# Two 512-wide tiles for the prompt, and a token-major product for the samples, in a decoder's input projection

## The chip, the core and the metric

The kernel runs on one core of one Trainium2 chip. The core has five engines that run side by side, each through its own queue in order: TensorE (PE, matrix products into PSUM, with its weight loads as PEld), VectorE (DVE), ScalarE (ACT, activations and casts), GpSimd (POOL) and SyncE (SP), which here issues the DMAs. The metric is the time of one execution in microseconds (us).

## The reference

One layer of a decoder in fp32 with 1024 prompt tokens and 32 sample tokens (8 sequences of 4), width 1024. One input projection feeds two groups of 512 channels: an HGRN2 recurrence with four heads, and a gated depthwise convolution of width 31 with a layer norm. An output projection merges them; then come the residual and a final RMSNorm.

```python
h = rmsnorm(x, norm_g)
proj = h @ w_in                                   # 1024 -> 3584
q, fp, i, za, glu, zb = jnp.split(proj, [s1, s2, s3, s4, s5], axis=-1)
q = silu(q); f = lb + (1 - lb) * sigmoid(fp); k = 1 - f; logf = log(f)
o_a, s_new = hgrn2_chunked(heads(q), heads(k), heads(i), heads(logf), s0)
o_a = rmsnorm(o_a, a_norm_g) * silu(za)
u = (glu + b_glu)[..., :512] * sigmoid((glu + b_glu)[..., 512:])
cv, buf_new = causal_dwconv(u, conv_buf, conv_w, conv_b)
o_b = silu(layernorm(cv, ln_g, ln_b)) * silu(zb)
out = x + concatenate([o_a, o_b], -1) @ w_out     # then the final rmsnorm
```

The same layer runs over the prompt (from a zero state) and over the samples (from given states).

## The kernel before

**Input.** `prep_x` normalizes 128 tokens at a time, turns them on PE and splits them into a high and a low part (type float32r), so that three fast products, high x high, high x low and low x high, stand in for one of fp32. The result is `xT`: channels in partitions, 1056 tokens (1024 of the prompt, then the 32 samples) in columns. `xsT` keeps the 32 sample tokens unsplit. `v_block` makes the values `i` token-major; `col_tiles` makes those of the samples by plain fp32 products that place the 32 tokens in one of four groups of 32 output partitions.

**Projections.** The other 24 blocks of 128 output channels are made feature-major, in the order of `ORD` (gb, ga: the two halves of the GLU; f, q; then za, zb). `load_w` fetches a block's weights into `wraw` (two buffers), and ScalarE and VectorE split them into `wh` and `wl`. `project` runs over three tiles of MB = 352 columns (3 x 352 = 1056), 24 matmuls each (8 slices of the contraction, three products), each tile in a PSUM bank of the tag `mm` (4 banks). Then it evacuates the banks, the third first (`nbs=(2, 0, 1)`), with an activation or a VectorE operation that `evac` makes; `after` chains them, and `lnexp_after` asks for the table set of logarithm and exponential behind the last.

**What sets the order.** `pump`, called behind the first and the second tile and at the end, emits pieces of the recurrence (`hgrn`, up to HU = 3 a call) and of background work (convolution `conv`, layer norm `ln_main`), as long as VectorE's sum of estimated costs lags PE's by less than LEAD. A scheduler then orders the instructions of each engine by its own estimate of the time; the pieces marked `high_priority` come first among those that can start. Each engine's queue runs strictly in the order that results.

**Memory.** `big` tiles (4 x 1056 columns) share six buffers: four of `xT`, the split weights of `i` (later `mixa`) and `cv`; later the output weights and the residual reuse them. PSUM: `mm` 4 banks, `aux` 2, `ops` 1, `ptps` 1.

Nearly every VectorE and PE instruction goes through the helper `Clock`, so in the profile its line is L72 (L73 after the change), and tiles tell instructions apart. The recurrence of the sample tokens has a group that the prediction uses: eight plain fp32 products of `qz` (32 columns of weights) with `s0` (tag `raw`, 128 moving columns), in the four column groups, into an `aux` bank (L645 to L654); a plain fp32 product `ops<-pt,vt` (L558) is another.

Of the kernel before, what the change touches and what calls it, by code (L numbers as in the profile page):

```python
# [18 lines left out]
P = 128  # L19
# [6 lines left out]
MB = 352  # L26
KO = 8
# [17 lines left out]
# columns of the packed per-partition vectors  # L45
# [9 lines left out]
# masks: causal, then s/t pairs of each level 64..1, then the diagonal  # L55
# [33 lines left out]
def _pe_ns(name, a, k):  # L89
    rhs = k.get("rhs")  # L90
    n = _free(a[0])
    if rhs is None:
        return 109
    return max(107, n / 2.4) if rhs.dtype == F32R else max(60, 4 * n / 2.4)


def emit(nc, tc, h, fast, flag_out=None):
    HW = 6 if fast else 5
    with ExitStack() as ctx:
# [8 lines left out]
        def big(dt=F32, w=TOK):  # L108
            return pool.tile([P, 4, w], dt, tag="big", name="big", bufs=6)
# [4 lines left out]
        def mmbank():  # L114
            return bank("mm", 4)
# [19 lines left out]
        xT = [[big(F32R) for _ in range(2)] for _ in range(2)]  # [hi/lo][ko half]  # L135
# [5 lines left out]
        xsT = sb([P, KO, ST], "ho", 2)  # L141
# [11 lines left out]
        def prep_x(tb, xr, n):  # L153
            sq = sb([P, 1], "ss", 4)
            junk = sb([P, D], "hw", HW, BF16)
            S.activation(junk[0:n, :], xr[0:n, :], AF.Square, accum_out=sq[0:n, :])  # L156
            S.activation(sq[0:n, :], sq[0:n, :], AF.Ln, bias=eps[0:n, :], scale=1.0 / D)  # L157
            S.activation(sq[0:n, :], sq[0:n, :], AF.Exp, scale=-0.5)
            V.scalar_tensor_tensor(
                xr[0:n, :], xr[0:n, :], sq[0:n, :], gin[0:n, :], ALU.mult, ALU.mult  # L160
            )
            for hf in range(2):
                tp = aux() if hf else mmbank()
                for k in range(4):
                    ko = hf * 4 + k
                    T.transpose(
                        tp[:, k * n : (k + 1) * n],
                        xr[0:n, ko * P : (ko + 1) * P],
                        ident[0:n, 0:n],
                    )  # L170
                src = tp[:, 0 : 4 * n].rearrange("p (k t) -> p k t", t=n)
                hi = xT[0][hf][:, :, tb * P : tb * P + n]
                S.copy(hi, src)  # L173
                if tb == 8:
                    S.copy(xsT[:, 4 * hf : 4 * hf + 4, :], src)
# [95 lines left out]
        # queries of the sample tokens, one zero-padded group of columns for each sequence  # L271
# [8 lines left out]
        # lower bound of the forget gate: first row of the softmax over the logits  # L280
# [25 lines left out]
        def load_w(blk):  # L306
            with tc.high_priority(HP):
                wr = sb([P, KO, P], "wraw", 2)
                nc.sync.dma_start(wr, h["win"][blk])
                hi = sb([P, KO, P], "wh", 2, F32R)  # L310
                lo = sb([P, KO, P], "wl", 2, F32R)
                S.copy(hi, wr)  # L312
                V.tensor_tensor(lo, wr, hi.bitcast(F32), ALU.subtract)
            return hi, lo
# [28 lines left out]
        def pump():  # L343
            for _ in range(HU):
                step(hq)
            while bg and V.ns < T.ns + LEAD * 1000:
                step(bg)
# [35 lines left out]
        def act_into(dst, func, bias=0.0):  # L383
            def f(nb, ps):
                return [S.activation(dst[:, nb * MB : (nb + 1) * MB], ps, func, bias=bias)]  # L385
# [7 lines left out]
        def hgrn(hd, q, k, g):  # L393
# [4 lines left out]
            for hf in range(2):  # L398
# [44 lines left out]
                # decayed keys towards the chunk's end, token-major  # L443
# [155 lines left out]
            # the four groups of partitions hold the parts (hi, hi, lo, lo) of the keys and  # L599
            # (hi, lo, hi, lo) of the values, so one product carries all four pairs  # L600
# [101 lines left out]
        def conv(c, u):  # L702
# [61 lines left out]
        def glu_evac(u, func, bias):  # L764
            us = u[:, UW:UEND].rearrange("p (b t) -> p b t", t=PAD + NS)

            def f(nb, ps):
                n = min(MB, SEQ - nb * MB)
                parts = [(u[:, PAD + nb * MB : PAD + nb * MB + n], ps[:, 0:n])]
                if n < MB:  # L770
                    parts.append((us[:, :, PAD:], ps[:, n:MB].rearrange("p (b t) -> p b t", t=NS)))
# [90 lines left out]
        for i, (kind, c) in enumerate(order):  # L862
# [23 lines left out]
            elif kind == "ga":  # L886
# [8 lines left out]
                if c == 3:  # L895
# [5 lines left out]
                    bg.append(ln_main())  # L901
# [24 lines left out]
            else:  # L926
# [14 lines left out]
                elif c == 3:  # L941
# [5 lines left out]
                        (0, 1, 2),  # L947
# [22 lines left out]
        for ko in range(KO):  # L970
# [11 lines left out]
            else:  # L982
                if ko == 4:
                    hi1 = big(F32R, D)
                    lo1 = big(F32R, D)
# [13 lines left out]
        def newton(y, v):  # L999
            # one step for y = v ** -0.5; v is used up  # L1000
# [63 lines left out]
        def finish(tb, pss):  # L1064
            if tb % 4 == 0:
                xres["t"] = big(w=D)
# [28 lines left out]
        pss = [[mmbank(), mmbank()] for _ in range(2)]  # L1095
# [123 lines left out]
```

## Time and profile before

| what | value |
|---|---|
| median of 3 runs | 519.52 us (519.48 to 519.6) |
| span of the profiled execution | 517.7 us |
| median less that span | 1.8 us |
| mean granted TensorE clock | 0.990 |
| matmuls 352 wide into `mm` | 1728 |
| projections | 24 |

The page gives the span from the first to the last instruction; it has no time of its own for what lies around the span, so the runs' median stands for it. The trace tells of each instruction when it started, how long it was at work, and what ended the engine's idle time before it. Matmuls are pipelined: their durations overlap, and the distance from one start to the next is what a matmul costs the engine. A plain fp32 product is recorded as two matmuls. The chain of work is followed back from the last instruction to what released it, or to the one before it on its engine; its pieces are runs of one engine and tile. In a table of stages each row has, for PE, PEld, DVE, ACT and POOL, the busy time and the count of instructions, then the granted clock, the share of the DMA engines and GB/s.

### The profile page before, as it was taken

Reading aid. Unit: us, or ns where it says so; the run is one execution under the profiler, and the core shown is the slowest. Engines: PE = TensorE matmul, PEld = TensorE weight load, DVE = VectorE, ACT = ScalarE, POOL = GpSimd, SP = SyncE. Lnnn points to the kernel's source line nnn. Section 1 sums busy time; section 2 is a strip of 40 time slices with the busy share of each in tenths; the row PEclk is TensorE's granted clock in tenths of the full one; section 3 lists DMA queues with packets and bytes.
Section 4 is the critical chain, followed back from the end, with each engine's and each line's share of the span. In section 5 each row is a group of like instructions: output and inputs, shape, how many; then the busy total and the mean of one; then the engine's idle time right before and its main releaser. Section 6 shows DMA issues by size and latency. Waiting matters only on the chain.

```text
span 517.7 us, 8480 instructions
## 1 busy us (share of the span) xinstructions
PE 502.1 (97%) x3404; PEld 453.2 (88%) x3404; DVE 384.0 (74%) x721; ACT 275.6 (53%) x517; POOL 2.9 (1%) x20
## 2 busy tenths in 40 slices
PE   5999999999999999999999999999999999999992
PEld 5789999889999999989999999999999967788881
DVE  4872299998988369998999989979566767545432
ACT  5873343213866475654737644754757868343321
POOL 1000000000000000000000000000000000000000
PEclk9899999999999999999999999999999999999997
DMA  8734122200211204111151001221125370211111
GB/s 303 241 136 100 42 52 50 43 0 1 51 42 43 55 22 114 41 42 47 42 122 47 22 37 47 88 76 42 47 56 185 128 304 33 87 46 42 63 58 47
DMA packets 21854, 39.37 MB, mean 76 GB/s; under 512 B 10512, under 2 KB 11792, under 8 KB 21808
## 3 DMA queue, kind: packets, MB, share of 16 engines
q1 hardware_dynamic: 21808, 38.77, 24.2%
q8 instruction: 28, 0.46, 0.4%
q14 instruction: 18, 0.15, 0.1%
HBM read 31.52 MB, written 7.24 MB: 75 GB/s over the span
## 4 chain that ended last, share of the span: by engine, by line
PE 94%; DMA 2%; ACT 2%; DVE 1%; SPq 1%; issue 0%; DVEq 0%
PE mm L72 73%; PE ops L72 8%; PE ptps L72 8%; PE aux L72 5%; DMA wl<-wi 2%; ACT hw L156 1%; DVE qkg L72 0%; SPq L216 0%; ACT big L173 0%; ACT big L224 0%; SPq L150 0%; ACT ss L157 0%; ACT big L1078 0%; ACT qkg L1089 0%; DVE cq L72 0%
## 5 line engine op out<-in xcount | busy, mean ns | idle before, releaser
L72 PE MATMUL mm<-big,wh 128*128 128x352 f32 (+1 forms) x1280 | 325.0, 332 | 0.0
L72 PEld LDWEIGHTS mm<-big,wh 128*128 128x128 f32 x1280 | 224.2, 188 | 7.1 <-issue 0.4
L72 PE MATMUL mm<-big,wl 128*128 128x352 f32 (+1 forms) x640 | 212.4, 332 | 0.0
L72 PEld LDWEIGHTS mm<-big,wl 128*128 128x128 f32 x640 | 120.5, 188 | 3.8 <-issue 0.4
L72 DVE SCALAR_TENSOR_TENSOR big<-u,wsum,big 128x511 f32<-128x511 f32 (+14 forms) x60 | 44.3, 739 | 0.3
L72 DVE TENSOR_TENSOR wl<-wraw,wh 128x1024 fp32r<-128x1024 f32 x24 | 29.3, 1222 | 20.6 <-ACT wh L312 20.5
L72 DVE SCALAR_TENSOR_TENSOR big<-u,cols,big 128x511 f32<-128x511 f32 (+14 forms) x60 | 44.1, 737 | 0.0
L72 DVE SCALAR_TENSOR_TENSOR cq<-u,cols,cq 128x511 f32<-128x511 f32 (+13 forms) x56 | 41.1, 734 | 0.0
L385 ACT ACTIVATE qkg<-mm 128x352 f32<-128x352 f32 x48 | 19.2, 465 | 31.7 <-PE mm L72 31.6
L312 ACT CAST wh<-wraw 128x1024 fp32r<-128x1024 f32 x24 | 25.2, 1050 | 19.0 <-PE mm L72 10.3
L72 DVE TENSOR_TENSOR qkg<-mm,big 128x512 f32<-128x512 f32 x16 | 10.9, 689 | 30.9 <-PE mm L72 30.9
L72 DVE TENSOR_TENSOR hw<-hw,qkg 128x512 f32<-128x512 f32 (+1 forms) x64 | 32.7, 550 | 0.0
L72 PE MATMUL ops<-big 128*128 128x512 f32 (+1 forms) x128 | 26.4, 399 | 1.7 <-ACT big L224 1.7
L325 ACT ACT_TABLE_LOAD x20 | 25.7, 1283 | 0.3
L72 PE MATMUL mm<-vt,wl 128*128 128x512 f32 x64 | 25.0, 391 | 0.0
L72 PE MATMUL mm<-vt,wh 128*128 128x512 f32 x64 | 25.0, 393 | 0.0
L1078 ACT ACTIVATE big<-qkg 128x512 f32<-128x512 f32 x16 | 10.0, 628 | 23.7 <-DVE qkg L72 23.7
L72 PEld LDWEIGHTS ptps<-hw 128*32 128x32 f32 (+1 forms) x448 | 13.7, 113 | 8.6 <-issue 3.4
L72 PE MATMUL ptps<-big 128*128 128x512 f32 x64 | 20.9, 395 | 0.4 <-ACT big L173 0.4
L72 PEld LDWEIGHTS ops<-big 128*128 128x128 f32 (+1 forms) x128 | 14.8, 155 | 5.9 <-ACT big L224 1.9
L72 PE MATMUL ptps<-hw 128*32 128x32 f32 (+1 forms) x448 | 19.7, 210 | 0.0
L385 ACT ACT_TABLE_LOAD x15 | 19.2, 1283 | 0.7 <-DVE hw L72 0.4
(226 smaller groups left out, 682.0 us busy)
## 6 DMA issues: line engine op xcount, KB each, us to landing
wraw<-win SPq DMA_DIRECT2D x24, 512.0 KB, 3.7
big<-xp SPq DMA_DIRECT2D x2, 2048.0 KB, 10.0
o_yp<-qkg SPq DMA_DIRECT2D x16, 256.0 KB, 2.3
wraw<-wo SPq DMA_DIRECT2D x6, 512.0 KB, 3.8
raw<-sh SPq DMA_DIRECT2D x4, 512.0 KB, 5.5
o_hs<-raw SPq DMA_DIRECT2D x4, 512.0 KB, 2.7
wh<-xp SPq DMA_DIRECT2D x3, 512.0 KB, 10.1
raw<-xp SPq DMA_DIRECT2D x2, 512.0 KB, 5.1
```

Source lines behind the costliest of these rows:

```text
L72: return f(*a, **k)
L156: S.activation(junk[0:n, :], xr[0:n, :], AF.Square, accum_out=sq[0:n, :])
L312: S.copy(hi, wr)
L325: after(S.preload_act_table_set("natural_log_exp_and_others"), prev)
L385: return [S.activation(dst[:, nb * MB : (nb + 1) * MB], ps, func, bias=bias)]
L1078: S.activation(xr[:, hs], y[:, hs], AF.Square, accum_out=sqs[:, half : half + 1])
```

## The change

`project` now makes the prompt's 1024 columns in two tiles of TB = 512, and the 32 sample columns apart:

- Eight plain fp32 products into a bank of its own (`smp`, one buffer; `mm` has three) take the unsplit weights `w[2]` (`wraw`) as the moving operand and `xsT` as the weights, 32 tokens in each of four groups of partitions, two slices of the contraction summed in each group. The result is token-major: four partial sums of 32 tokens x 128 channels.
- ScalarE copies that to `sps`, and one fp32 product with `bones` (ones where two partitions mean the same token) sums the four parts and turns them to 128 channels x 32 tokens, in other columns of the `smp` bank.
- The third "tile" that `evac` sees is that 32-column piece. The order of evacuation is 0, 1, 2 everywhere.
- `pump` is called behind the sample group, in the second tile behind its fourth slice (after the turning product), and at the end.

`load_w` returns the unsplit weights too, so `wraw` stays in use until PE has read it. `xT` has 1024 columns and a tag of its own (`xt`, four buffers; `big` has two); the output weights and the residual that reused `big` now reuse `xt`. The sample tokens aren't split any more in `prep_x`, and `xsT` has its own tag. `step` and `pump` hold the layer norm's generator until all four heads are done. The cost estimate of a matmul gains 13 (or 10) ns. The first two output tiles of the output product use three `mm` banks and `smp`. Comments are gone, so line numbers differ.

```diff
-            return bank("mm", 4)
+            return bank("mm", 3)
+
+        def smpbank():
+            return bank("smp", 1)
...
+                if tb == 8:
+                    S.copy(xsT[:, 4 * hf : 4 * hf + 4, :], src)
+                    continue
                 hi = xT[0][hf][:, :, tb * P : tb * P + n]
                 S.copy(hi, src)
-                if tb == 8:
-                    S.copy(xsT[:, 4 * hf : 4 * hf + 4, :], src)
...
         def step(q):
-            while q:
+            while q and not (q[0] is late.get("ln") and len(hdone) < H):
...
-        def project(w, evac, ndrain, nbs=(2, 0, 1), more=()):
+        def project(w, evac, ndrain, more=()):
             pss = []
-            for nb in range(3):
+            smp = smpbank()
+            for nb in range(2):
                 ps = mmbank()
                 i = 0
                 for ko in range(KO):
                     for a, b in ((0, 0), (0, 1), (1, 0)):
                         T.matmul(
-                            ps[:, 0:MB],
+                            ps,
                             lhsT=w[b][:, ko, :],
-                            rhs=xT[a][ko // 4][:, ko % 4, nb * MB : (nb + 1) * MB],
+                            rhs=xT[a][ko // 4][:, ko % 4, nb * TB : (nb + 1) * TB],
                             start=(i == 0),
                             stop=(i == 23),
                         )
                         i += 1
+                    if nb == 1 and ko == 3:
+                        T.matmul(
+                            smp[:, P : P + ST], lhsT=sps, rhs=bones[:, 0:ST], start=True, stop=True
+                        )
+                        if ndrain:
+                            pump()
                 pss.append(ps)
-                if nb < 2 and ndrain:
-                    pump()
+                if nb == 0:
+                    for ko in range(KO):
+                        j = ko % 4
+                        T.matmul(
+                            smp[j * ST : (j + 1) * ST, 0:P],
+                            lhsT=xsT[:, ko, :],
+                            rhs=w[2][:, ko, :],
+                            start=(ko < 4),
+                            stop=(ko >= 4),
+                            tile_position=(0, j * ST),
+                        )
+                    sps = sb([P, P], "sps", 2)
+                    S.copy(sps, smp[:, 0:P])
+                    if ndrain:
+                        pump()
+            pss.append(smp[:, P : P + ST])
             with tc.high_priority(HP):
                 last = None
-                for nb in nbs:
-                    for ins in evac(nb, pss[nb][:, 0:MB]):
+                for nb in range(3):
+                    for ins in evac(nb, pss[nb]):
```

How the order of PE's queue changes, at the projection ga0 (the second one). Before, at the end of a tile (a row is a line, an operation, output<-inputs by the program's names with their numbers, and the output's shape; `mm_501` is the bank of the tile, `big` is `xT`, `wh` and `wl` the split weights, `ops` and `ptps` the banks of `v_block`):

```order
L72 MATMUL mm_501<-big_77,wh_408 128x352
L72 MATMUL mm_501<-big_77,wl_409 128x352
L72 MATMUL mm_501<-big_79,wh_408 128x352
L72 MATMUL ops_865<-qkg_164,big_77 128x512
L72 MATMUL ops_865<-big_80,big_79 128x512
L72 MATMUL ptps_891<-big_80,big_76 128x512
```

The tile ends, and other products of the same fast type follow at once. After, ga0's second tile goes into `mm_519` (`xt` is `xT`, `smp_483` the sample bank, `wraw` the unsplit weights, `xsT` the sample tokens):

```order
L73 MATMUL mm_519<-xt_76,wh_404 128x512
L73 MATMUL mm_519<-xt_76,wl_405 128x512
L73 MATMUL mm_519<-xt_78,wh_404 128x512
L73 MATMUL smp_483<-wraw_402,xsT_84 32x128 x8
L73 MATMUL mm_519<-xt_76,wh_404 128x512
L73 MATMUL mm_519<-xt_76,wl_405 128x512
L73 MATMUL mm_519<-xt_78,wh_404 128x512
```

The eight sample products stand behind the first three matmuls of the second tile. 21 matmuls of 512 columns further on, already in the first tile (`mm_560`) of the next projection, follows the product that turns them:

```order
L73 MATMUL mm_560<-xt_76,wh_479 128x512
L73 MATMUL mm_560<-xt_76,wl_480 128x512
L73 MATMUL smp_483<-bones_374,sps_517 128x32
L73 MATMUL mm_560<-xt_78,wh_479 128x512
L73 MATMUL mm_560<-xt_76,wh_479 128x512
```

So the copy to `sps` has that stretch of PE's queue to be done in. Most of the 24 projections read alike; in seven the group of eight is cut in two by other matmuls.

The other place is ScalarE's queue around the third q block (c = 2). Before (`qkg<-mm` is the evacuation of a projection, ACT_TABLE_LOAD the load of a table set):

```order
L694 ACTIVATE big<-aux,eps 128x512
L695 ACTIVATE big<-big 128x512
L385 ACT_TABLE_LOAD
L385 ACTIVATE qkg<-mm 128x352 x3
L325 ACT_TABLE_LOAD
L312 CAST wh<-wraw 128x1024
```

The three tiles are evacuated in one batch between two table loads. After, at the same projection:

```order
L727 ACTIVATE big<-ops 128x512
L421 ACT_TABLE_LOAD
L421 ACTIVATE qkg<-mm 128x512
L482 ACT_TABLE_LOAD
L482 ACTIVATE eg<-qkg 128x4
L398 COPY sps<-smp 128x128
```

The first tile is evacuated by itself, and the set of the exponential (`eg`) is loaded again before the copy and before the second tile. In the whole fast path ScalarE's queue has 44 table loads before and 79 after.

More of the change, by code (lines that the diff above doesn't have):

```diff
@@ L106, in sb, with big @@
             return pool.tile(shape, dt, tag=tag, name=tag, bufs=bufs)
-        def big(dt=F32, w=TOK):
-            return pool.tile([P, 4, w], dt, tag="big", name="big", bufs=6)
+        def big(dt=F32, w=TOK, tag="big"):
+            return pool.tile([P, 4, w], dt, tag=tag, name=tag, bufs={"big": 2, "xt": 4}[tag])
         def bank(tag, bufs):
@@ L132, in emit @@
         nc.vector.tensor_copy(avgr, av)
-        xT = [[big(F32R) for _ in range(2)] for _ in range(2)]
+        xT = [
+            [big(F32R, SEQ, "xt") for _ in range(2)]
+            for _ in range(2)
+        ]
         wih = big(F32R, D).rearrange("p a (b n) -> p (a b) n", n=512)
@@ L346, in pump @@
             while bg and V.ns < T.ns + LEAD * 1000:
+                if bg[0] is late.get("ln") and len(hdone) < H:
+                    break
                 step(bg)
-        def project(w, evac, ndrain, nbs=(2, 0, 1), more=()):
+        def project(w, evac, ndrain, more=()):
             pss = []
-            for nb in range(3):
+            smp = smpbank()
+            for nb in range(2):
                 ps = mmbank()
@@ L384, in f @@
             def f(nb, ps):
[L385 removed]
+                return [
+                    S.activation(dst[:, nb * TB : min(TOK, (nb + 1) * TB)], ps, func, bias=bias)
+                ]
             return f
@@ L900, in emit @@
                     bg.insert(len(bg) - 1, lnp())
-                    bg.append(ln_main())
+                    late["ln"] = ln_main()
+                    bg.append(late["ln"])
             elif kind == "f":
@@ L1065, in finish @@
             if tb % 4 == 0:
-                xres["t"] = big(w=D)
+                xres["t"] = big(w=D, tag="xt")
                 nc.sync.dma_start(
@@ L1094, in emit @@
         mixes = [split_mix(0), split_mix(1)]
-        pss = [[mmbank(), mmbank()] for _ in range(2)]
+        pss = [[mmbank(), mmbank()], [mmbank(), smpbank()]]
         for kos in (range(4), range(4, KO)):
```

20 lines of the change are left out of this document (10 added, 10 removed).

## The prediction

> **What bounds the kernel now.** I read the share of each engine first, then the chain of work that ended last, then what TensorE waited for.
>
> ```profile
> span 517.7 us, 8480 instructions
> PE 502.1 (97%) x3404; PEld 453.2 (88%) x3404; DVE 384.0 (74%) x721; ACT 275.6 (53%) x517; POOL 2.9 (1%) x20
> ...
> PE 94%; DMA 2%; ACT 2%; DVE 1%; SPq 1%; issue 0%; DVEq 0%
> PE mm L72 73%; PE ops L72 8%; PE ptps L72 8%; PE aux L72 5%; DMA wl<-wi 2%; ACT hw L156 1%; DVE qkg L72 0%; SPq L216 0%; ACT big L173 0%; ACT big L224 0%; SPq L150 0%; ACT ss L157 0%; ACT big L1078 0%; ACT qkg L1089 0%; DVE cq L72 0%
> ```
>
> TensorE is 94% of the chain, and matmuls into the `mm` banks are 73%: the 24 projections and the output product. A busy PE could still hide waits, so the list of PE's waits comes next.
>
> ```profile
> PE ops L72 <- ACT big L224: 1.7, 1, 1.7
> PE mm L72 <- DVE avg L132: 1.6, 1, 1.6
> PE mm L72 <- DVE raw L72: 1.2, 1, 1.2
> PE ops L72 <- DVE qkg L72: 0.8, 1, 0.8
> PE ptps L72 <- ACT big L173: 0.4, 1, 0.4
> PE mm L72 <- ACT ho L175: 0.2, 1, 0.2
> ```
>
> These six waits sum to 5.9 us and are of the input stage (L132, L173, L224 build the transposed input). The table of stages says the same of the 296 us in which most projections and all recurrences run:
>
> ```profile
> 114.00:410.00 296.00, 296.00 (x2248) 279.93 (x2248) 247.58 (x470) 179.47 (x329) 0.25 (x2) 1.00 0.20 56
> 180.00:340.00 160.00, 160.00 (x1230) 150.07 (x1229) 143.60 (x281) 96.66 (x186) 0.00 (x0) 1.00 0.21 57
> ```
>
> PE is busy for every microsecond, at the full granted clock; VectorE for 248 and ScalarE for 179. So what the change is worth is, first, what it does to the sum of PE's own spacings. Durations of single matmuls (some 330 ns) overlap and are no price; the price is the time from start to start.
>
> **The tiles.** A projection had 3 x 24 matmuls 352 wide and gets 2 x 24, 512 wide. The chain has an unbroken run of each shape:
>
> ```profile
> 56.66 22.97 PE mm L72 x144
> ...
> 449.91 58.25 PE mm L72 x256
> ```
>
> 22.97 / 144 = 159.5 ns for 352 columns, 58.25 / 256 = 227.5 ns for 512 (the output product). Before: 72 x 159.5 = 11.48 us. After: 48 x 227.5 = 10.92. That saves 0.56 us; with the starts below (160 ns between neighbours) it is 72 x 160 - 48 x 227 = 0.62. I take 0.60, or **-14.4 us** for 24 projections (13.5 to 15.0). Most comes from the 24 matmuls fewer (their fixed part: 227 - 160 = 67 ns buys 160 columns, 0.42 ns each, so 12 to 13 ns of the 160 are fixed), the rest from 32 of 1056 columns.
>
> **The sample group.** Eight plain fp32 products, weights 128x32, 128 moving columns, into four column groups. The old kernel has exactly this form in the recurrence of the sample tokens (`aux<-raw,qz`, recorded as 16, two records each), and once it stands alone among 352-wide matmuls:
>
> ```profile
> 254.88 0.32 PE L72 MATMUL mm<-big,wl 128*128 128x352 f32 x1
> 255.13 0.64 PE L72 MATMUL aux<-raw,qz 128*32 128x128 f32 x16
> 255.70 0.59 PE L72 MATMUL mm<-big,wh 128*128 128x352 f32 x2
> 256.13 0.32 PE L72 MATMUL mm<-big,wl 128*128 128x352 f32 x1
> ```
>
> From 254.88 to 256.13 are 1.25 us, in which three plain 352-wide matmuls (0.48) start too: the group costs **0.77 us**; I use 0.78. Only some 0.48 of it is the group's own records; the rest is the switch of form, paid going in (0.25 to the first record where 0.16 is usual) and coming out. The way in is no wait for data, since it is the same before other column-tiled groups:
>
> ```profile
> 153.04 0.32 PE L72 MATMUL mm<-big,wh 128*128 128x352 f32 x1
> 153.29 0.33 PE L72 MATMUL ptps<-hw 128*64 128x64 f32 x2
> ```
>
> Again 0.25. The other instance took a little more:
>
> ```profile
> 188.41 0.42 PE L72 MATMUL mm<-big,wh 128*128 128x352 f32 x1
> 188.77 0.64 PE L72 MATMUL aux<-raw,qz 128*32 128x128 f32 x16
> 189.34 0.43 PE L72 MATMUL mm<-big,wl 128*128 128x352 f32 x1
> ```
>
> 0.93 from matmul to matmul against 0.82 above: 0.88 for the upper end. 24 x 0.78 = **+18.7 us** (11.5, without any switch, to 21.1).
>
> **The turning product.** One plain fp32 product, 128x128 weights and 32 moving columns. Its nearest row alone among 352s is the fp32 product of 128 moving columns, two records:
>
> ```profile
> 277.78 0.32 PE L72 MATMUL mm<-big,wh 128*128 128x352 f32 x1
> 277.94 0.38 PE L72 MATMUL ops<-pt,vt 128*128 128x128 f32 x2
> 278.08 0.41 PE L72 MATMUL mm<-big,wh 128*128 128x352 f32 x1
> 278.33 0.32 PE L72 MATMUL mm<-big,wl 128*128 128x352 f32 x1
> ```
>
> 277.78 to 278.33 is 0.55 us; without it 0.32; so 0.23, and fewer columns need not help, since the two records start 0.11 apart. 24 x 0.225 = **+5.4 us** (0.14 to 0.30 each). The new order also cuts seven of the 24 groups in two; two pieces stand far apart and pay the switch again: 2 x 0.3 = **+0.6** (0 to 2.1).
>
> PE's sum: -14.4 + 18.7 + 5.4 + 0.6 = **+10.3 us**. The saving is smaller than the work that replaces it: 0.60 against 1.00 us a projection.
>
> A rule of the Trainium skill speaks about the fixed part: the page TensorEngine Tiling (Array Packing), section Performance Considerations, Instruction Overhead, gives every matmul about 60 cycles of overhead, 25 ns at the 2.4 GHz that it assumes. By it the tiles would save more and the sum would be some 7 us smaller; the rows of 159.5 and 227.5 ns put the fixed part at half of that, and they decide.
>
> **What lies beside PE.** ScalarE gains 24 copies of `smp`, and the evacuation changes from three of 352 to two of 512 and one of 32.
>
> ```profile
> L656 ACT COPY kts<-aux 128x128 f32<-128x128 f32 x4 | 1.0, 255 | 3.3 <-PE aux L72 3.3
> L385 ACT ACTIVATE qkg<-mm 128x352 f32<-128x352 f32 x48 | 19.2, 465 | 31.7 <-PE mm L72 31.6
> L1078 ACT ACTIVATE big<-qkg 128x512 f32<-128x512 f32 x16 | 10.0, 628 | 23.7 <-DVE qkg L72 23.7
> L325 ACT ACT_TABLE_LOAD x20 | 25.7, 1283 | 0.3
> ```
>
> A projection: 3 x 0.465 = 1.40 before; 2 x 0.628 + 0.28 + 0.26 = 1.79 after; 9 us more in all. Larger is what the order does: the first tile no longer waits for the last, so its activation is issued mid-projection, and other tables come between. ACT_TABLE_LOADs go from 44 to 79: 35 x 1.283 = 45 us. In 114 to 410 us ScalarE would go from 179 to about 230 of 303 us. It has the room: 116 us idle there, and the evacuations alone waited 31.6 us for PE. What matters is whether a late copy holds `smp<-bones,sps`, since PE's queue goes no further. The order puts that product 21 matmuls behind the group: 21 x 0.227 = 4.8 us. Before it ScalarE has, at the third q block, an activation (0.63), a table (1.28), a small exponential (0.2) and the copy (0.26): 2.4 us from the end of the first tile. Covered by 2 us; with a second table or a late VectorE operand it would not be. I price that at **+1.7 us**, about one table load and a bit exposed in all 24, with 0 and 22 us (half of the 45) as ends.
>
> The weights' raw tile is now read by PE, so the load two blocks on (SP's queue, 3.7 us) waits for the group. It was free after VectorE's split; now it is free mid-projection, with 5.4 us of that projection and the whole next one still to run before its first use. Behind it on SP stand state loads and outputs, needed later still. Three banks and a fourth suffice, since two are held and the third takes the next tile. Sample columns leave the hi/lo split of the input: four short operations fewer on ScalarE and VectorE, none of them on PE. I cost all this at nothing; if the cover went, one late weight load would cost up to its 3.7 us.
>
> The sum: 10.3 + 1.7 = **+12.0**. The profiled execution's span is 517.7; the runs' median 519.52 has 1.8 around it, which I carry unchanged: **531.5 us**.
>
> **Rivals.**
> - *ScalarE's tables surface.* Place: the recurrence stage, where VectorE too is at 143.6 of 160 us and each late exponential idles it. A third to a half of the 45 us: +10.3 + 15 to 22, 545 to 552, decided where ScalarE's backlog exceeds the 2 us above. Against it: PE had no wait there before, ScalarE idles 39%. 0.22.
> - *The switch isn't paid.* Place: both ends of each sample group. If groups cost their records alone (0.48) and the product 0.14, the sum is 24 x (0.62 - 0.60) = +0.5, 520.0: not slower. It decides when both cost under 0.64 us together. Against it: 0.25 us or more on the way in, three times above. 0.05.
> - *A larger fixed part.* If 25 of the 160 ns were fixed, 512 columns would take 25 + 512 x 135 / 352 = 221 ns and the tiles save 0.91 a projection: 24 x (1.00 - 0.91) + 0.6 + 1.7 = +4.5, 524.0. The 256 matmuls at 227.5 speak against it. This is the rule of the page named above. 0.03.
>
> **How the numbers follow.** Forecast 0.68 (527 to 537), tables 0.22, no switch 0.05, larger fixed part 0.03, and 0.02 for a gain that I don't see. The range 526 to 545 leaves out half of the tables' case and the small ones, about 0.2. Measurement tells about 0.2% from no change. Slower by more: 0.93; within: 0.04 (most of the no-switch case); faster: 0.03.
>
> **What would show it.** In the profile after: PE still over 95% busy; 1152 projection matmuls 227 ns apart; from the last 512 before a sample group to the second after it 0.78 us more than three plain starts; the turning product 0.2; 79 table loads and some 330 us of ScalarE, with no row `PE smp <- ACT sps` over 2 us in the list of waits. Such a row of 10 us, or PE waiting for `hw` or `pt`, means that the tables surfaced. Starts at 0.23 on both sides of a group mean that the switch isn't paid, and I am wrong by 7 us or more.

## The result, and the profile after

| | before | after |
|---|---|---|
| median of 4 runs | 519.56 us (519.48 to 519.66) | 539.67 us (539.08 to 541.47) |
| ratio, 95% interval | | 1.0391 (1.0374 to 1.0409) |
| span of the profiled execution | 517.7 us | 537.3 us |
| table loads on ScalarE | 44 | 79 |

Slower by 20.1 us, where 12.0 was forecast: inside the range, 8 us from the number. Two runs far above their neighbours, of 820.69 us (e6_before_012) and 1248.16 us (before), are left out of all medians here and below. The page of the changed kernel, its shares and its chain:

```profile
span 537.3 us, 8266 instructions
...
PE 516.8 (96%) x3260; PEld 407.1 (76%) x3260; DVE 383.8 (71%) x715; ACT 326.9 (61%) x570; POOL 2.9 (1%) x20
...
PE 81%; ACT 9%; DVE 5%; DMA 3%; issue 1%; SPq 0%; ACTq 0%; DVEq 0%
```

TensorE is still 96% busy; ScalarE's 327 us and the 79 table loads are as forecast. But the chain is now 81% TensorE, where it was 94%. The list of TensorE's waits (line waited for, sum in us, times, longest):

```profile
PE aux L73 <- ACT cq L869: 2.1, 1, 2.1
PE ops L73 <- ACT xt L183: 1.7, 1, 1.7
PE mm L73 <- DVE raw L73: 1.7, 1, 1.7
PE mm L73 <- DVE avg L136: 1.6, 1, 1.6
PE ops L73 <- DVE big L73: 1.3, 1, 1.3
PE aux L73 <- DVE st L73: 1.2, 1, 1.2
PE ops L73 <- DVE xt L73: 0.6, 1, 0.6
PE mm L73 <- ACT xsT L180: 0.5, 1, 0.5
```

They sum to 10.7 us, against 5.9 before. The new ones are `cq` (layer norm), `big` and `st` (recurrence); no row has `smp` waiting for `sps`. The table of stages, in the two windows of the prediction and the one behind them:

```profile
114.00:410.00 296.00, 293.46 (x2044) 228.76 (x2043) 230.71 (x443) 213.61 (x356) 0.25 (x2) 1.00 0.18 52
180.00:340.00 160.00, 158.79 (x1108) 123.33 (x1100) 136.12 (x259) 115.97 (x193) 0.00 (x0) 1.00 0.19 51
410.00:450.00 40.00, 37.86 (x215) 27.98 (x214) 29.80 (x40) 32.05 (x46) 0.00 (x0) 0.96 0.56 200
```

TensorE, full in every microsecond before, has small gaps in both stages and a larger one in 410 to 450, where the granted clock falls too (0.96). By 410 us VectorE has done 230.7 where it had done 247.6: the work is late.

**TensorE's sum.** To keep work and waits apart, I took from the trace of before the median distance from start to start for each pair of neighbouring forms of matmul, and added these along each kernel's own order (for the sample group, those of `aux<-raw,qz`). The true time from the first start to the last, less this sum, is the excess. It holds what waits and a lowered clock cost, and also whatever the spacings of a new order differ from those of before:

| kernel | TensorE's sum | true | excess | last `ptps<-hw` | third `cq<-u` | span | median |
|---|---|---|---|---|---|---|---|
| before | 499.5 | 506.1 | 6.7 | 364.1 | 420.2 | 517.7 | 519.6 |
| after | 509.6 | 525.7 | 16.1 | 377.4 | 441.0 | 537.3 | 539.7 |
| e1_batch | 509.6 | 529.6 | 20.0 | 381.5 | 443.7 | 541.2 | 542.4 |
| e2_last2 | 508.4 | 520.4 | 12.0 | 377.7 | 437.6 | 532.0 | 535.1 |
| e3_nogroup | 491.6 | 532.0 | 40.4 | 381.5 | 447.1 | 544.5 | 543.9 |
| e8_whole | 504.6 | 533.5 | 28.8 | 385.4 | 448.9 | 545.1 | 547.1 |
| e3c_nogroup | 491.2 | 529.5 | 38.3 | 379.8 | 445.6 | 542.0 | 542.7 |
| e4c_tiles | 479.8 | 524.2 | 44.4 | 371.7 | 440.1 | 535.8 | 538.0 |
| e6_before_012 | 499.6 | 516.0 | 16.5 | 371.0 | 431.7 | 527.7 | 529.8 |
| e10_first | 505.9 | 526.2 | 20.3 | 376.6 | 441.8 | 537.9 | 541.0 |
| f2_tiles_batch | 480.7 | 527.0 | 46.3 | 378.2 | 442.4 | 538.6 | 540.8 |
| f5_late_batch | 508.3 | 536.8 | 28.6 | 386.5 | 452.8 | 548.4 | 550.8 |
| h1_tiles_conv | 482.1 | 517.7 | 35.6 | 366.5 | 432.5 | 529.4 | 531.3 |
| h2_after_conv | 508.0 | 520.9 | 12.8 | 362.1 | 431.2 | 532.5 | 534.6 |

(us; the two columns of starts are explained with the second bound below.) The sum rose by 10.1, the excess by 9.4.

A second account needs no spacings of before. From the same true time I take TensorE's idle time, and what a lowered clock took from its busy time (the busy time multiplied by one less the granted clock, in pieces of 0.1 us). The rest is TensorE's own work at full clock, together with waits too short to show as idle:

| kernel | idle | lost to the clock | rest |
|---|---|---|---|
| before | 4.5 | 1.7 | 500.0 |
| after | 9.3 | 3.3 | 513.0 |
| e1_batch | 9.1 | 7.2 | 513.2 |
| e2_last2 | 6.2 | 2.9 | 511.3 |
| e3c_nogroup | 27.2 | 13.1 | 489.2 |
| e4c_tiles | 28.9 | 13.7 | 481.6 |
| h2_after_conv | 5.4 | 3.2 | 512.3 |

By it the idle time rose by 4.8 us, the loss to the clock by 1.6 and the rest by 13.0. So some 3 of the 9.4 us of excess are not idle time: they are longer spacings of the new order, or waits hidden behind the pipelined matmuls; which of the two is open. They stand in the recurrence: from 180 to 410 us the excess rose by 6.4, with 2.5 us of idle time and a clock of 1.00.

### The profile page after: what moved, and what is told of

The parts are those of the page before. It is cut to its first block, busy times and chain, and to the rows that moved or that the text cites. A ratio compares the mean times of both kernels' runs of the same rounds, so it can differ in the third digit from the quotient of the medians.

```text
span 537.3 us, 8266 instructions
## 1 busy us (share of the span) xinstructions
PE 516.8 (96%) x3260; PEld 407.1 (76%) x3260; DVE 383.8 (71%) x715; ACT 326.9 (61%) x570; POOL 2.9 (1%) x20
## 4 chain that ended last, share of the span: by engine, by line
PE 81%; ACT 9%; DVE 5%; DMA 3%; issue 1%; SPq 0%; ACTq 0%; DVEq 0%
PE mm L73 59%; PE ops L73 7%; PE ptps L73 7%; PE aux L73 5%; PE smp L73 4%; DVE big L73 2%; DMA wraw<-wi 1%; DVE hw L73 1%; ACT hw L163 1%; DMA raw<-wo 1%; ACT L421 1%; DVE qkg L73 1%; DMA wraw<-wo 1%; ACT big L232 1%; ACT vt L1025 1%
## 5 line engine op out<-in xcount | busy, mean ns | idle before, releaser
L73 PE MATMUL mm<-xt,wh 128*128 128x512 f32 x888 | 291.0, 399 | 0.0
L73 PEld LDWEIGHTS mm<-xt,wh 128*128 128x128 f32 x888 | 165.6, 188 | 38.0 <-issue 4.8
L73 PE MATMUL mm<-xt,wl 128*128 128x512 f32 x444 | 176.0, 396 | 0.0
L73 PEld LDWEIGHTS mm<-xt,wl 128*128 128x128 f32 x444 | 83.6, 188 | 15.9 <-issue 0.2
L73 DVE SCALAR_TENSOR_TENSOR big<-u,wsum,big 128x511 f32<-128x511 f32 (+14 forms) x60 | 44.4, 739 | 0.5
L73 DVE SCALAR_TENSOR_TENSOR big<-u,cols,big 128x511 f32<-128x511 f32 (+14 forms) x60 | 44.4, 739 | 0.0
L73 DVE TENSOR_TENSOR qkg<-mm,xt 128x512 f32<-128x512 f32 x15 | 10.4, 691 | 32.4 <-PE mm L73 32.4
L421 ACT ACTIVATE qkg<-mm 128x512 f32<-128x512 f32 x32 | 19.0, 597 | 13.2 <-PE mm L73 13.0
L1115 ACT ACTIVATE xt<-qkg 128x512 f32<-128x512 f32 x16 | 10.1, 629 | 26.1 <-DVE qkg L73 26.1
L73 PE MATMUL ops<-big,xt 128*128 128x512 f32 x64 | 22.6, 418 | 2.4 <-ACT xt L183 1.7
L73 PEld LDWEIGHTS ptps<-hw 128*32 128x32 f32 (+1 forms) x448 | 14.0, 113 | 10.1 <-issue 3.3
L73 PE MATMUL ptps<-big,xt 128*128 128x512 f32 x64 | 20.6, 393 | 0.0
L1078 ACT CAST wh<-big 128x512 fp32r<-128x512 f32 x16 | 9.2, 617 | 17.3 <-PE mm L73 15.3
```

The costliest lines, as they stand in the source:

```text
L73: return f(*a, **k)
L421: S.activation(dst[:, nb * TB : min(TOK, (nb + 1) * TB)], ps, func, bias=bias)
L1078: S.copy(hv, m[:, :, ts])
L1115: S.activation(xr[:, hs], y[:, hs], AF.Square, accum_out=sqs[:, half : half + 1])
```

## The experiments

Three accounts stood for the excess: added table loads, output weights made late by the held `wraw`, and sample groups cut in two.

**e1_batch: the old order of evacuation.** (In the kernel before, the last projection, zb3, already had the order 0, 1, 2; here it has 2, 0, 1 too.)

```diff
-                for nb in range(3):
+                for nb in (2, 0, 1):
```

> The changed kernel with the three pieces of a projection evacuated in the old order (third, first, second) instead of first, second, third, so that all three activations come after the last product again. Table loads on ScalarE fall from 79 to 52; the sum of TensorE's starts stays (509.5 against 509.6 us). Three accounts of the 9 us by which the change cost more than TensorE's sum of +10.2. Tables: the 35 added loads of 1.28 us surfaced in front of TensorE; then most of the 9 us goes, 531 to 534. Weights: the weight tile that the sample group holds longer makes the output weights late; nothing here frees it, 539 to 540. Split groups: they stay split, 539 to 540.

Measured 542.38 us, ratio to before 1.0432 (1.0415 to 1.045): 27 table loads fewer, and 3 us slower than the change. A row of what ScalarE waited for, in 114 to 410 us, shows a new wait:

```profile
ACT sps L398 <- PE smp L73: 38.5, 11, 6.9
```

With the activations now behind the projection, the copy reaches the head of ScalarE's queue early and blocks it until TensorE has made the group. So this run takes loads away but adds a wait; it could not clear the loads, and f5 was made to. TensorE's idle time is the same as in the change (9.1 us against 9.3). What is longer is the loss to the clock, by 3.9 us: the granted clock was 0.94 in 260 to 340 us, where it was 1.00 in the change.

**e2_last2: no group in the last two projections.**

```diff
-        def project(w, evac, ndrain, more=()):
+        def project(w, evac, ndrain, more=(), samples=True):
...
+                    if samples:
+                        for ko in range(KO):
...
+                        S.copy(sps, smp[:, 0:P])
+                    else:
+                        sps = vs
...
+                        samples=False,
```

> The changed kernel, but the last two projections (zb2, zb3) leave out their sample group; the turning product there reads another tile, so the sample columns of those two blocks are not computed. Their weight tiles are free as early as before the change, and the output weights can be loaded then. TensorE's sum falls by 1.4 us (508.2 against 509.6). Weights: the 4.9 us by which TensorE falls behind its own sum in 410 to 450 us mostly go too, 533.5 to 535.5. Tables: they stay 79, only the sum's part goes, 538 to 538.5. Split groups: the same, 538 to 538.5.

Measured 535.11 us, ratio 1.0305 (1.0288 to 1.0322): 4.6 us less than the change, of which 1.2 is TensorE's sum. The loads of the output weights on SP's queue, in before, after and this run (count, durations, first and last start):

```profile
L973 SPq DMA_DIRECT2D wraw<-wo x6: 327/328/437, 370.8 to 425.3; - x6
```

```profile
L1010 SPq DMA_DIRECT2D wraw<-wo x6: 327/328/372, 407.4 to 443.7; - x6
```

```profile
L1015 SPq DMA_DIRECT2D wraw<-wo x6: 328/328/340, 393.7 to 430.8; - x6
```

The change started the first of them 37 us later; with `wraw` free earlier it starts 14 us sooner again. The excess in 410 to 450 us falls from 4.9 to 1.1 (before: 1.8), and no other stage changes by over 0.3. The weights account holds, for 3.8 us. How late weights reach TensorE shows in the chain of after, between 422 and 443 us:

```profile
422.28 5.22 DMA raw<-wo
...
429.16 1.28 ACT L333
...
433.00 1.64 DVE big L73
...
441.00 0.49 ACT cq L869
```

One load of the output weights (into `raw`, behind late ones into `wraw` on SP's queue) holds up a cast on ScalarE, behind which the layer norm stands in the same queue; for its `cq` TensorE then waited the 2.1 us of the list above, and ran at a lowered clock behind that wait. In e2 that wait is 0.2 us.

**e3_nogroup and e3c_nogroup: no sample group at all.** Group and copy go; the last line, which keeps the planner's count of TensorE's time, stands in e3c alone.

```diff
-                    for ko in range(KO):
-                        j = ko % 4
-                        T.matmul(
...
-                    sps = sb([P, P], "sps", 2)
-                    S.copy(sps, smp[:, 0:P])
+                    sps = vs
+                    T.ns += 8 * (4 * P / 2.4 + 10)
```

> The changed kernel without any sample group and without its copy; the turning product stays and reads another tile, so the sample columns of all projections are not computed. TensorE's sum falls by 18.2 us (491.4 against 509.6), which contains the split groups. Table loads 70. Only the sum counts: 521.5. Weights and split groups (all of what hangs on the group goes with it): 513 to 516, the waits back near those of before. Tables: 9 of the 35 added loads go, so most of the 9 us stay, 519 to 521.

> The run without sample groups came out slower than the changed kernel although TensorE's sum fell by 18 us. In it the planner's count of TensorE's time, by which the background work is dealt out, also lost the group (8 x 223 = 1.8 us a projection). Here the group and its copy are left out again (sample columns not computed), but the count is kept as in the changed kernel. TensorE's sum 491.1. If the pace of the planner made that run slow: 515 to 522 (sum, span's rest and waits as in the changed kernel or fewer). If VectorE's and ScalarE's chains are a second bound that TensorE's groups merely covered: still 537 to 545, with waits of TensorE of 20 us or more for DVE and ACT in 290 to 312 and 410 to 450 us.

Measured 543.86 us, 1.0455 (1.0433 to 1.0477), and 542.69 us, 1.0429 (1.0402 to 1.0456). TensorE has 18 us less to do, and both are slower than the change. The three accounts fell: the excess took back all of the saving and more. The pace of the planner falls too: its count moves the time by 1 us. What e3c bears out is the account of a second bound (537 to 545).

**e8_whole: no cut groups.**

```diff
+                    with tc.high_priority(HP):
                         for ko in range(KO):
```

> The changed kernel with the eight products of a sample group emitted at a higher priority, so that nothing is put between them: 24 whole groups in place of 31 pieces. TensorE's sum falls by 5.1 us (504.5 against 509.6) by the transitions of the trace. Split groups: the time falls by about that, 533.5 to 535.5. Tables (still 79) and weights (tile held until about the same point): the waits stay, so they also expect the sum's part, but if the seven splits cost only the 0.6 us that was forecast, 538 to 539.5.

Measured 547.06 us, 1.0528 (1.051 to 1.0546). The sum fell by 5.0 as worked out, the excess rose by 12.7; of its 28.8 us, 9.2 stand in 260 to 340 and 8.6 in 410 to 450 us. So TensorE's own work is some 5 us less with whole groups, and more than that is lost elsewhere.

**e4c_tiles: the two tiles alone.** Neither group nor copy nor turning product; the third piece is read from another tile.

```diff
-            pss.append(smp[:, P : P + ST])
+            pss.append(vs[:, 0:ST])
```

> The two 512-wide tiles alone: neither group nor copy nor turning product; the third piece is evacuated from another tile, so the sample columns of the projections are not computed; the planner's count is kept as in the changed kernel. TensorE's sum 479.6 against 509.5 in the changed kernel and 499.3 in the kernel before. If TensorE alone bounds: 502 to 508, faster than before by the 14.4 us of the tiles and the third product that they spare. If VectorE's and ScalarE's chains are a second bound: 525 to 545, no better than the changed kernel by more than 10.

Measured 538.03 us, 1.0349 (1.0327 to 1.0371). TensorE has 30 us less to do than in the change, and the time falls by 1.6. TensorE's longest waits in it, and two of its stages:

```profile
PE aux L73 <- ACT cq L855: 5.4, 1, 5.4
PE ops L73 <- DVE big L73: 4.8, 2, 3.9
PE mm L73 <- ACT wh L1064: 4.6, 1, 4.6
PE ops L73 <- DVE st L73: 3.9, 2, 3.4
PE ptps L73 <- DVE hw L73: 2.6, 2, 1.9
```

```profile
180.00:340.00 160.00, 148.82 (x903) 117.93 (x901) 147.86 (x279) 103.80 (x180) 0.00 (x0) 0.95 0.16 50
410.00:450.00 40.00, 26.09 (x135) 18.64 (x134) 29.30 (x41) 30.87 (x42) 0.00 (x0) 0.83 0.41 158
```

TensorE now idles 11 us in the recurrence's stage, where VectorE is at 147.9 of 160, and 14 us of the 40 behind it. Its clock is lowered there too (0.95 and 0.83; in the change 1.00 and 0.96). So two things took the saving back: 24.4 us more idle time than in the kernel before, and 12.0 us more lost to the clock, against 18.4 us less work (the second account). With the clock loss of before, and this idle time unchanged, it would still be some 512 us from first start to last, 6 over the kernel before (an estimate from these sums). So there is a second bound: TensorE waits for other engines for longer than the saving. It is no fixed time: e3, e3c and e4c have spans of 536 to 545 us, and e2, with some 29 us more of TensorE's work than the tiles alone, has 532.

**e6_before_012: the kernel before, evacuated first, second, third.**

```diff
-        def project(w, evac, ndrain, nbs=(2, 0, 1), more=()):
+        def project(w, evac, ndrain, nbs=(0, 1, 2), more=()):
```

> The kernel before, with its three tiles evacuated first, second, third instead of third, first, second: the activation is issued mid-projection, and table loads on ScalarE go from 44 to about 99, some 70 us more of ScalarE, while TensorE's sum stays (499.4). Tables surface behind VectorE (ScalarE late, VectorE idle, TensorE late): 525 to 540. Tables are covered: 519 to 520.5.

Measured 529.81 us, ratio 1.0198 (1.0174 to 1.0223), with 99 table loads. The new waits:

```profile
PE aux L72 <- ACT ho L460: 3.7, 1, 3.7
...
PE aux L72 <- ACT cq L832: 1.6, 1, 1.6
...
PE aux L72 <- ACT ho L689: 1.4, 1, 1.4
```

The order of evacuation alone, one line of the change, costs the kernel before 9.9 us (519.9 beside it) with TensorE's sum unchanged; the excess grew by 9.8.

**e10_first: the group ahead of the first tile.**

```diff
             smp = smpbank()
+            for ko in range(KO):
+                j = ko % 4
+                T.matmul(
...
+            sps = sb([P, P], "sps", 2)
+            S.copy(sps, smp[:, 0:P])
             for nb in range(2):
```

> The changed kernel with the sample group ahead of the first tile of its projection instead of between the tiles; all is computed. The weight tile is free half a projection earlier, the copy of smp is in time for the product, and TensorE's sum falls to 505.8 (fewer cut groups). Held weights: the tail's waits shrink too, 531 to 535. Only the sum: 535.5 to 536. If the waits hang on how the new order meets VectorE and ScalarE, as in the run with whole groups: anything from 536 to 547, with waits in 290 to 312 us.

Measured 541.03 us, 1.0412 (1.0395 to 1.0429). The sum fell by 3.7, the excess rose by 4.2; it stands at 7.0 in 260 to 340 and at 6.3 in 410 to 450 us.

**f2_tiles_batch and f5_late_batch: is it the table loads?** The tiles alone with all evacuation behind the last product; and the whole change with the old order and a late copy, behind the recurrence's work of the planner.

```diff
-                for nb in range(3):
+                for nb in (1, 0, 2):
```

> The two tiles alone, as before (no group, copy or turning product; sample columns of the projections not computed; planner's count kept), but evacuated second, first, third, so that every activation comes after the projection's last product, as in the kernel before. Table loads fall to about the kernel before's 44. TensorE's sum 480.6. If the evacuation in the order of the tiles (table loads, late casts of weights, VectorE idle behind them) sets the bound near 538 that the tiles alone ran into: 500 to 512. If the bound lies elsewhere (three mm banks, the order of the recurrence): 530 to 540.

```diff
+                    if nb == 1 and ko == 1:
+                        sps = sb([P, P], "sps", 2)
+                        S.copy(sps, smp[:, 0:P])
...
-                for nb in range(3):
+                for nb in (2, 0, 1):
```

> The whole changed kernel, evacuated third, first, second, and with the copy of smp emitted in the second tile (after its sixth product of 24) and the turning product behind that tile. In the first run with this evacuation order ScalarE stood 38.5 us behind copies that waited for their group; here the recurrence's work of the planner is ahead of the copy. TensorE's sum 508.1, about 45 table loads. If order of evacuation and blocked copies were what kept that run slow: 523 to 530. If the bound lies elsewhere: 538 to 545.

Measured 540.78 us, 1.041 (1.0392 to 1.0429), and 550.78 us, 1.061 (1.0579 to 1.064). Both have 47 table loads, about the 44 of before, and neither gains. ScalarE's copies still blocked it in f5 (31.4 us in 114 to 410), so f5 is no clean test. f2 has no copies, but its first tile is evacuated later than in the tiles alone. So it shows that 20 loads fewer don't by themselves bring the time back; what a load costs, apart from that delay, it doesn't show.

**h1_tiles_conv and h2_after_conv: is it VectorE's amount of work?** 48 of the convolution's 192 operations are left out, in the tiles alone and in the whole change.

```diff
-            for i in range(14, -1, -1):
+            for i in range(14, 3, -1):
...
-            for i in range(14, -1, -1):
+            for i in range(14, 3, -1):
```

> The two tiles alone (538.0 us; no group, copy or turning product, planner's count kept), and 12 of the 48 taps' operations of each channel block of the convolution left out too, so that its output lacks those taps: 48 of VectorE's 192, some 35 us at 0.737 each, none of it TensorE's. TensorE's sum 482.0, table loads unchanged. If VectorE's queue is the second bound (its 317 us of work before the second layer-norm block, plus its idle time): 538 - 35 = 503, or what TensorE's sum allows with the waits of the kernel before, 482 + 20 = 502. If the bound is ScalarE's tables, the banks or the weights: 530 to 538.

> The whole changed kernel with the same 48 operations of the convolution left out on VectorE; group, copy and product as in the change. TensorE's sum 507.9. If VectorE's queue made the 9 us that the change cost beyond TensorE's sum: the sum with the waits and the rest of the kernel before, 507.9 + 6.7 + 13.4 = 528, or 531 with the late output weights still there. If VectorE is no bound: 536 to 539.

Measured 531.28 us, 1.0215 (1.0198 to 1.0233), and 534.61 us, 1.0289 (1.0265 to 1.0314). Some 35 us of VectorE's work (48 at 0.737) are worth 6.8 us in the tiles alone: its amount is not the bound by itself, though it plays a part. In the whole change it is worth 5.1 us, 1.6 of them TensorE's sum by another order. That run has no wait over 1.3 us behind the input stage.

Freed of most waits, the changed kernel takes 534.6, 3 us over the forecast of 531.5; its excess, in pieces under 2.5 us a stage behind the input, is still 6.1 above that of before. By the second account only 0.9 of that is idle time and 1.5 the clock; TensorE's rest is 12.3 us above that of before, where the sum is 8.5. So with TensorE nearly always busy the new order costs it more than the sums of spacings say.

## The second bound

What is common to all fourteen kernels shows in the rows of one PSUM bank, `ptps`. The last product of the last head's prompt recurrence writes it (`ptps<-hw`), and it has one buffer, which the layer norm's means (`ptps<-cq`) use next. In the changed kernel and all made from it, the generator of the layer norm is also held until the four heads are done. Rows of the tile in a window around that place (count, durations min/median/max in ns, first and last start), before, after, and with the tiles alone:

```profile
L72 PE MATMUL ptps<-hw x4: 196/206/217, 364.0 to 364.1; 128*32 128x32 f32 x4
...
L72 PE MATMUL ptps<-cq,avg x2: 404/406/407, 368.9 to 369.3; 128*128 128x352 f32 x2
```

```profile
L73 PE MATMUL ptps<-hw x28: 196/196/270, 376.5 to 377.4; 128*32 128x32 f32 x24, 128*64 128x64 f32 x4
...
L73 PE MATMUL ptps<-cq,avg x2: 318/363/408, 382.9 to 383.1; 128*128 128x352 f32 x2
```

```profile
L73 PE MATMUL ptps<-hw x12: 196/197/217, 370.3 to 371.7; 128*32 128x32 f32 x12
...
L73 PE MATMUL ptps<-cq,avg x2: 323/324/325, 376.9 to 377.1; 128*128 128x352 f32 x2
```

The first mean follows 3.7 to 5.5 us behind the last `ptps<-hw` in every kernel. Three blocks of layer norm follow one another, and in TensorE's queue the second half of the output product stands behind the third block. The row of the three blocks' casts on ScalarE, before and after (the last start is the third's):

```profile
L832 ACT CAST cq<-u x3: 474/483/485, 375.6 to 420.2; 128x352 fp32r<-128x352 f32 x3
```

```profile
L869 ACT CAST cq<-u x3: 480/484/486, 390.8 to 441.0; 128x352 fp32r<-128x352 f32 x3
```

From the last of these to the end of the span are 94.4 to 97.5 us in thirteen of the fourteen kernels (101.3 in h2, where TensorE holds the end up). That alone would not say who waits for whom, since the kernel before has this interval too, and no wait in front of it. The waits say it: in eleven of the fourteen (all but before, e1 and h2) TensorE idled for the third block's `cq`, 0.2 us in e2, 1.6 in e6, 2.1 in after, 5.4 in the tiles alone and 8.1 in f5. In these the end hangs on a series: four heads' recurrences through all three engines, the layer norm, the rest of the output product. The table's columns of starts read so: in the change the recurrence ended 13.3 us later and what lies behind it took 6.3 longer (159.9 against 153.6), together the 19.6 by which the span grew. In the tiles alone the recurrence ended 7.6 later, although TensorE had 20 us less to do than before.

In the kernel before this chain was covered, as TensorE had no waits behind the input stage. How far below TensorE's bound it lay is open: the run that would tell, the kernel before with less for TensorE, was not made. Open too is which part of the new order holds the chain in the tiles alone: the three `mm` banks for four, the other places of `pump`, the held layer norm, the changed cost estimate, or the wider tiles. None was tried by itself. Only the order of evacuation was, in the kernel before (9.9 us, e6).

## Why the forecast came out as it did

- **The bound.** "what the change is worth is, first, what it does to the sum of PE's own spacings" is the step that did not hold. A TensorE that is full tells that it is a bound, not that it is the only one. Taking 18 to 30 us from its sum (e3, e3c, e4c) changed the time by +4.2, +3.0 and -1.6 us; even with sample columns for nothing it would have stayed at 538. That the forecast came within 8 us all the same is in part luck, since the two bounds lie close: TensorE's sum with the waits and the rest of the kernel before gives 509.6 + 6.7 + 13.4 = 529.7, the tiles alone measured 538.
- **The tiles, -14.4.** Right. The 512-wide matmuls start 227 ns apart, in the trace of after as in the output product of before: 24 x (48 x 227 - 72 x 160) ns is -15 us. The sum of the tiles alone is 19.7 us under that of before; the rest goes with fewer changes between the fast products and others in its order (149 against 191).
- **The sample group, +18.7, and the turning product, +5.4.** Right. Rows of after around a whole group and around a product:

```profile
258.86 0.39 PE L73 MATMUL mm<-xt,wh 128*128 128x512 f32 x1
259.18 0.64 PE L73 MATMUL smp<-wraw,xsT 128*32 128x128 f32 x16
259.76 0.50 PE L73 MATMUL mm<-xt,wh 128*128 128x512 f32 x1
260.10 0.40 PE L73 MATMUL mm<-xt,wl 128*128 128x512 f32 x1
```

```profile
62.04 0.40 PE L73 MATMUL mm<-xt,wl 128*128 128x512 f32 x1
62.27 0.31 PE L73 MATMUL smp<-bones,sps 128*128 128x32 f32 x2
62.41 0.71 PE L73 MATMUL mm<-xt,wh 128*128 128x512 f32 x2
```

  From 258.86 to 260.10 are 1.24 us with two plain starts (0.454) in them: 0.78, as forecast, and so is the median of the seventeen places where a whole group stands between 512-wide matmuls. The product is 0.236 by the median of its places, against 0.225. The way into the group is 0.32 where 0.227 is usual.
- **Cut groups, +0.6 (0 to 2.1).** Too small, if anything: with whole groups TensorE's sum is 5.0 lower (e8). Not all of that need be the cuts, since the rest of the order moved too.
- **PE's sum, +10.3.** Worked out as +10.1 along the new order, and +13.0 by the second account. That forecast and sum agree to 0.2 is luck: the tiles alone took 19.7 off where 14.4 were forecast, and group, product and cuts added 29.8 where 24.7 were. Two errors of 5 us cancel.
- **ScalarE's waits, +1.7 (0 to 22).** Mis-sized, and in the wrong place. No row has the turning product `smp<-bones,sps` waiting for its copy. TensorE's idle time rose by 4.8 instead, in front of `st`, `big` and `cq`, and the clock took 1.6 more. The excess, which also holds the longer spacings, rose by 9.4, spread over the recurrence and the tail: +1.6 in 180 to 260, +2.4 in 260 to 340, +2.4 in 340 to 410, +3.1 in 410 to 450 us, +0.5 in the input stage, and -0.6 in the rest.
- **The held weight tile, costed at nothing.** Wrong, by about the amount given for that case: "one late weight load would cost up to its 3.7 us"; e2 shows 3.8. That the two agree is luck: it was no single load of 3.7 us, but late loads that held ScalarE, and through it the layer norm, and in the end a wait of 2.1 us with slow matmuls behind it. The loads named as its cover were the next projection's; the output weights, which need the same two buffers at the end, were not looked at.
- **Rival: ScalarE's tables surface.** Right in its place ("the recurrence stage, where VectorE too is at 143.6 of 160 us") and wrong in its measure. One such case stands in the chain of after:

```profile
372.12 1.28 ACT L421 ACT_TABLE_LOAD   x1
...
374.02 1.28 ACT L731 ACT_TABLE_LOAD   x1
...
376.18 1.28 ACT L732 ACT_TABLE_LOAD   x1
```

  Three loads in 5.4 us ahead of `big`, for which TensorE then waited 1.3 us. But with 47 loads in place of 67 the tiles alone lost another 2.8 us (f2), so the count of loads alone doesn't set the time; their order against the recurrence may.
- **Rivals: the switch isn't paid, a larger fixed part.** Both fell: 0.32 into the group, and 227 ns where a fixed part of 25 would have given 221. The overhead of about 60 cycles that the Trainium skill gives in TensorEngine Tiling (Array Packing), section Performance Considerations, Instruction Overhead, was read in the prediction as a part added to every matmul; so read, it doesn't fit these rows. That section gives the cycles without a clock, and goes on to say that one column takes as long as 60, which is rather a least time; rows of 352 and 512 columns don't test that.

## What to carry to other kernels

Before pricing a change by the busiest engine's sum, make one run in which that engine has clearly less to do: if the time stays, a chain across the other engines is as long, and a saving there is worth nothing. Read the granted clock in that run too: here it was 0.96 in the mean where the changed kernel had 0.988, and part of the saving went there. Look for that chain at the tail, in a buffer with one copy that hands the last stage's work to the next (here the bank `ptps`), and follow who holds it. When an operand is kept in use longer, check every later user of its buffers, the next phase's loads above all, not only the next round of the same loop.

## What the hardware showed

A short wait was followed by slow matmuls. After TensorE's wait of 2.1 us at 441.54 the matmuls of 512 columns start 0.43 us apart, not 0.227, and the granted clock in the table of stages is half:

```profile
443.48 0.63 PE L73 MATMUL mm<-vt,wl 128*128 128x512 f32 x1
443.90 0.63 PE L73 MATMUL mm<-cq,wh 128*128 128x512 f32 x1
444.33 0.63 PE L73 MATMUL mm<-vt,wl 128*128 128x512 f32 x1
```

```profile
443.00:445.00 2.00, 2.00 (x5) 1.61 (x6) 1.90 (x4) 1.97 (x3) 0.00 (x0) 0.50 0.23 29
445.00:447.00 2.00, 2.00 (x9) 1.60 (x9) 0.84 (x1) 1.11 (x2) 0.00 (x0) 0.89 0.71 233
```

The full pace is back at about 446, so the 2.1 us of waiting cost nearly 2 us again. In after the two waits of 1.2 and 1.3 us at 307 and 379 had no such effect: the stage of 114 to 410 us shows a clock of 1.00. The length of a wait does not decide it alone: in e3c TensorE waited 3.6 us up to 420.91, and the clock was 1.00 in the stretch of 421 to 424 us; in h1 a wait of 1.5 us ended at 287.49, and the clock was 0.50 from 289.5 to 291. What decides it is open.
